# A two-layer transformer trunk: all four column blocks of the down projection by seven products in three blocks of a layer, two blocks' units in one order, one weight sum by adding DMAs

## The chip, the cores and the metric

The kernel runs on one core of one Trainium2 chip. The metric is the device time of one execution in microseconds (us), lower is better. Engines are named as the profile names them: PE (TensorE, matrix products), DVE (VectorE), ACT (ScalarE), POOL (GpSimd) and SP (SyncE, which here only issues DMAs).

## The reference, cut to what matters

256 tokens of width 2048 pass two layers. Each layer is a mixer (attention, not touched here) and an MLP with squared ReLU; the hidden width is 8192, everything is float32.

```python
def sq_relu_mlp(h, w_up, w_down):
    return jnp.square(jax.nn.relu(h @ w_up)) @ w_down

for layer in range(2):
    hn = rms_norm(h, ln_mix_g[layer])
    h = h + mixer(hn, ...)                      # even_mixer, then odd_mixer
    hn = rms_norm(h, ln_mlp_g[layer])
    h = h + sq_relu_mlp(hn, w_mlp_up[layer], w_mlp_down[layer])   # (2048, 8192), (8192, 2048)
```

## The kernel before, in words

**Units and splits.** All weights come as chunks of 1 MB by DMAs that SP issues into three buffers `raw`. A *unit* is 1024 columns of such a buffer, 128 partitions deep. For float32 accuracy each operand is cut into a high and a low part: `split` (L277, L280) lets ACT copy the unit into `wh` and lets DVE subtract, `wl = raw - wh`. PE then forms high·high, high·low and low·high, so that a product takes three matmuls, each 128x128 by 512 columns. There are `NHL` = 4 pairs `wh`, `wl`: unit u+3 is split while PE works on unit u, and ACT can begin that split only when PE has finished unit u-1. An ordinary unit is 12 matmuls.

**The order.** Everything is laid out in a Python list `units`; `run()` emits the units in that order, and between matmuls it lets background tasks (`bg`) emit a piece. Each engine executes its own instructions strictly in the order in which they were emitted, and waits at an instruction whose inputs aren't there. That holds for SP too: a DMA that waits for its buffer holds up every DMA behind it.

**The MLP.** The hidden width goes in eight blocks of 1024. `up_units(b)` makes block b of the hidden layer: 16 ordinary units, two groups g of 512 columns. The result lies token by token in PSUM; `blocks` (L440, DVE) and 16 small DMAs (`across`, L446, 32 KB each, issued by SP, `t<-t`) turn it into the layout that the next product needs; then L892 (DVE) squares the ReLU, and L899 (ACT) and L901 (DVE) cut it into high and low part in `big`.

**The down projection of block b** (0 to 6) is done in two ways. Column blocks 2 and 3 (of four, 512 columns each) by `pair_units(b)`: 8 ordinary units, 96 matmuls. Column blocks 0 and 1 by `seven_units(b)`, a Strassen-Winograd scheme: tokens, hidden rows and columns are halved, and seven products of sums take the place of eight. Each product is two units of 6 matmuls, so 84 matmuls in place of 96. The sums of hidden values are made by `token_sums`. The sums of weights are made in place: four 1 MB buffers (the three `sum` and `sm`) are loaded with the quarters x0, z0, w0, y0 of the weights, and a class `Stage` adds them up as their turn comes: x1 = x0 + w0, x2 = x1 + y0, y1 = y0 + w0, x3 = x2 + z0. Each of these sums is two additions on DVE (L236, 128x1024), one for each unit. A stage keeps the conditions `free` (its buffer may be overwritten), `have` and `used`; `run()` calls `issue` of all stages before each unit. After each of the seven products DVE adds the result to the residual `xs` (L983), of which P and R are PSUM banks 0 and 2 (several products go there one after another), and Q is bank 1.

**The order of a block.** For block b the list takes the 24 ordinary units of `up_units(b)` and `pair_units(b-1)`, and sets the 14 units of `seven_units(b-1)` between them at places `at`: three ordinary units to each product. Block 7 of the down projection is done whole by `down_units`, at the end.

Of the kernel before, what the change touches and what calls it, by code (L numbers as in the profile page):

```python
# [148 lines left out]
def trunk_kernel(ctx: ExitStack, tc: tile.TileContext, x, w_up, w_down, even_w_in, even_w_out,  # L149
# [65 lines left out]
    class Stage:  # L215
# [2 lines left out]

        def __init__(self, buf, free, src=None, add=None, prev=None):
            self.buf, self.free, self.src, self.add, self.prev = buf, free, src, add, prev
# [643 lines left out]
    def mlp(layer, norm, nxt):  # L866
        up, down = w_up[layer], w_down[layer]
        NBLK = DFF // 1024

        def hid(b):  # L870

# [5 lines left out]
        def up_units(b):  # L877
            for g in range(2):
                def evac(hf, ps, g=g):
                    turned_, d = T[g], T[2 + g]  # L880
                    if b:
                        bg.need(heads["hid", b - 1, g])
                    blocks(turned_[:, hf * 512:(hf + 1) * 512], ps)

                    def rest():
                        if b:
                            yield (lambda: heads["sum", layer, b - 1].done)
# [12 lines left out]
                        yield 1  # L900
                        nc.vector.tensor_tensor(lo, q, h, ALU.subtract)  # L901
                        yield 1
                    if hf == 1:
                        heads["hid", b, g] = bg.spawn(rest(), 1)

                a_units(up, [(b * 1024 + g * 512, 512)], xl, list(range(KT)), evac,
                        lambda g=g: (bank[4 + 2 * g], bank[5 + 2 * g]), norm.need)

        def token_sums(b):

            yield (lambda: b == 0 or ("sums", b - 1) in passed)
            x11, x21, x12, x22 = (T[i][:, a:a + 512].rearrange("p (s j t) -> p j s t", s=4, j=4)
                                  for i in (2, 3) for a in (0, 512))
            p, q = SQ
            for i, dst, a, c, op in ((0, p, x21, x22, ALU.subtract), (1, q, p, x11, ALU.subtract),
                                     (3, p, x12, q, ALU.add), (2, q, x11, x21, ALU.subtract)):
                d, a, c = (t.rearrange("p (j s t) -> p j s t", s=4, j=4) if t is p or t is q else t for t in (dst, a, c))
                nc.vector.tensor_tensor(d, a, c, op)  # L920
                yield 2
# [6 lines left out]
        def seven_units(b, first):  # L928

            def w(r, n):
                return down[b * 1024 + r * 512:b * 1024 + r * 512 + 512, n * 512:n * 512 + 512].rearrange("(k p) c -> p k c", p=128)

            bx, by, bz = (summed[(i + 2 * b) % 3] for i in range(3))
            old = kept.get(b - 1)

            def gone(f):

                return f if b else lambda i: current[0] >= start[0] and all(t.done for t in norm.tasks.values())  # L940
# [9 lines left out]
            kept[b] = dict(x1=x1, x3=x3, y1=y1, z0=z0)  # L950
# [10 lines left out]
            P, Q, R = bank[0:3]  # L961
            out_ = []

            for n, (st, lhs, need, o, new, half, col, neg) in enumerate((
                    (x0, hx(0, 0), h0, P, True, 0, 0, 0), (z0, hx(4, 0), hd, Q, True, 0, 0, 0),
                    (x1, sx(0), sm, R, True, 1, 1, 0), (y0, sx(3), sm, R, False, 0, 1, 0),
                    (x2, sx(1), sm, P, False, 0, 1, 1), (y1, sx(2), sm, P, False, 1, 1, 1),
                    (x3, hx(4, 1), hd, P, False, 1, 0, 0))):
                for i in range(2):
                    def gen(u, n=n, i=i, lhs=lhs, need=need, o=o, new=new, half=half, col=col, neg=neg):  # L970
                        bg.need(*need())
                        h, lo = (t[u % NHL].rearrange("p (j c) -> p j c", j=2) for t in (wh, wl))
                        for j in range(2):
                            jj = 2 * i + j
                            nc.tensor.matmul(o, lhs(jj, 0), h[:, j], start=new and jj == 0, stop=False, skip_group_check=True)  # L975
                            nc.tensor.matmul(o, lhs(jj, 0), lo[:, j], start=False, stop=False, skip_group_check=True)  # L976
                            nc.tensor.matmul(o, lhs(jj, 1), h[:, j], start=False, stop=jj == 3, skip_group_check=True)  # L977
                            if jj == 3:
                                xd = xs[:, half, col * 512:col * 512 + 512]
                                f = 2 * neg + half  # L980
                                if b == 0 and n == 0:
                                    bg.need(norm.rtask)
                                nc.vector.scalar_tensor_tensor(xd, o, norm.r2[:, f:f + 1], xd, op0=ALU.mult, op1=ALU.add)  # L983
                                passed.update({("sums", b)} if n == 5 else {("seven", b)} if n == 6 else ())
                            yield

                    out_.append((st, i * 1024, 1024, gen, True))
# [4 lines left out]
        def used(b, g):  # L992

            if b == 0:
                return True
            if b == NBLK - 1:
                return ("sums", b - 1) in passed
            return ("low", b - 1) in passed if g == 0 else {("seven", b - 1), ("eight", b - 1)} <= passed

        start = [None]  # L1000
        kept = {}
# [50 lines left out]

        start[0] = len(units) + 5
        up_units(0)
        for b in range(1, NBLK):
            plain_ = taken(up_units, b) + taken(pair_units, b - 1)
            seven = seven_units(b - 1, b == 1)


            at = (1, 7, 10, 13, 16, 19, 22) if b == 1 else (3, 6, 9, 12, 15, 18, 21)  # L1060
            units.extend(plain_[:at[0]])
            for i, (a, e) in enumerate(zip(at, at[1:] + (len(plain_),))):
# [295 lines left out]
```

## Time and profile before

| | |
|---|---|
| time, median of 3 runs | 2208.41 us (2208.19 to 2209.19) |
| the profiled execution | 2210.6 us, of which the span of its instructions 2208.8 us |
| PE busy | 2201.8 us of the span |
| DVE busy | 1675.4 us |
| ACT busy | 1152.1 us |
| POOL busy | 41.4 us |
| granted TensorE clock | 1.00 |
| the two MLPs in the span | about 455 to 1110 us and 1560 to 2209 us |

The span is the time from the first to the last instruction of the program. A busy PE says only that matmuls follow each other closely; whether one waited is read from the waits and from the chain of work that ended last.

### The profile page before, as it was taken

Reading aid. Unit: us, or ns where it says so; the run is one execution under the profiler, and the core shown is the slowest. Engines: PE = TensorE matmul, PEld = TensorE weight load, DVE = VectorE, ACT = ScalarE, POOL = GpSimd, SP = SyncE. Lnnn points to the kernel's source line nnn. Section 1 sums busy time; section 2 is a strip of 40 time slices with the busy share of each in tenths; the row PEclk is TensorE's granted clock in tenths of the full one; section 3 lists DMA queues with packets and bytes.
Section 4 is the critical chain, followed back from the end, with each engine's and each line's share of the span. In section 5 each row is a group of like instructions: output and inputs, shape, how many; then the busy total and the mean of one; then the engine's idle time right before and its main releaser. Section 6 shows DMA issues by size and latency. Waiting matters only on the chain.

```text
span 2208.8 us, 27276 instructions
## 1 busy us (share of the span) xinstructions
PE 2201.8 (100%) x10037; PEld 1822.5 (83%) x10037; DVE 1675.4 (76%) x2223; ACT 1152.1 (52%) x1471; POOL 41.4 (2%) x28
## 2 busy tenths in 40 slices
PE   9999999999999999999999999999999999999999
PEld 7788888888888888888888888888888888888887
DVE  5676766669888888888764676766788888888885
ACT  5555555545555554555543556555455555545553
POOL 0000000000000000000000000000000000000000
PEclk9999999999999999999999999999999999999999
DMA  8655655686675675675566664535765665765754
GB/s 269 192 190 177 188 182 197 186 274 206 225 243 179 217 247 163 224 238 171 172 194 198 222 201 133 165 110 177 240 232 174 231 227 168 241 227 176 238 171 153
DMA packets 281989, 442.74 MB, mean 200 GB/s; under 512 B 24704, under 2 KB 81280, under 8 KB 281856
## 3 DMA queue, kind: packets, MB, share of 16 engines
q1 hardware_dynamic: 280848, 439.89, 61.1%
q8 instruction: 78, 1.28, 0.2%
q10 hardware_dynamic: 1008, 1.12, 0.1%
q14 instruction: 55, 0.45, 0.1%
HBM read 410.52 MB, written 2.10 MB: 187 GB/s over the span
## 4 chain that ended last, share of the span: by engine, by line
PE 92%; DMA 3%; DVE 2%; SPq 1%; ACT 1%; issue 1%; POOL 0%; DVEq 0%; ACTq 0%
PE bank L376 47%; PE bank L363 8%; PE bank L364 8%; PE bank L365 8%; PE bank L977 4%; PE bank L975 4%; PE bank L976 4%; DMA raw<-in_odd_w_in 2%; PE bank L688 1%; PE bank L720 1%; DVE wl L280 1%; SPq L446 1%; DMA raw<-in_w_up 1%; PE bank L715 1%; PE bank L396 1%; PE bank L397 1%
## 5 line engine op out<-in xcount | busy, mean ns | idle before, releaser
L280 DVE TENSOR_TENSOR wl<-raw,wh 128x1024 fp32r<-128x1024 f32 (+1 forms) x659 | 797.9, 1217 | 313.6 <-ACT wh L277 303.1
L277 ACT ACTIVATE wh<-raw 128x1024 fp32r<-128x1024 f32 (+1 forms) x659 | 691.8, 1055 | 515.8 <-PE bank L376 268.7
L376 PE MATMUL bank<-wh,xT 128*128 128x512 f32 x2592 | 725.6, 391 | 0.0
L376 PEld LDWEIGHTS bank<-wh,xT 128*128 128x128 f32 x2592 | 485.1, 188 | 99.1
L376 PE MATMUL bank<-wl,xT 128*128 128x512 f32 x1296 | 406.3, 391 | 0.6 <-DVE wl L280 0.6
L277 ACT ACTIVATE wh<-sum 128x1024 fp32r<-128x1024 f32 x196 | 207.7, 1060 | 247.6 <-PE bank L376 159.1
L376 PEld LDWEIGHTS bank<-wl,xT 128*128 128x128 f32 x1296 | 243.2, 188 | 51.3 <-DVE wl L280 1.0
L280 DVE TENSOR_TENSOR wl<-sum,wh 128x1024 fp32r<-128x1024 f32 x196 | 238.9, 1219 | 57.3 <-ACT wh L277 57.3
L376 PE MATMUL bank<-wh,big 128*128 128x512 f32 x784 | 222.8, 391 | 0.0
L363 PE MATMUL bank<-wh,big 128*128 128x512 f32 x440 | 175.4, 399 | 0.0
L376 PEld LDWEIGHTS bank<-wh,big 128*128 128x128 f32 x784 | 146.9, 188 | 30.0
L365 PE MATMUL bank<-wh,big 128*128 128x512 f32 x440 | 171.6, 390 | 0.0
L364 PE MATMUL bank<-wl,big 128*128 128x512 f32 x440 | 171.4, 389 | 0.0
L363 PE MATMUL bank<-wh,xT 128*128 128x512 f32 x432 | 170.8, 395 | 0.1
L364 PE MATMUL bank<-wl,xT 128*128 128x512 f32 x432 | 168.4, 390 | 0.3 <-DVE wl L280 0.3
L365 PE MATMUL bank<-wh,xT 128*128 128x512 f32 x432 | 168.3, 390 | 0.0
L977 PE MATMUL bank<-wh,big 128*128 128x512 f32 x392 | 152.6, 389 | 0.0
L975 PE MATMUL bank<-wh,big 128*128 128x512 f32 x392 | 152.5, 389 | 0.0
L976 PE MATMUL bank<-wl,big 128*128 128x512 f32 x392 | 152.5, 389 | 0.0
L376 PE MATMUL bank<-wl,big 128*128 128x512 f32 x392 | 123.2, 392 | 0.0
L365 PEld LDWEIGHTS bank<-wh,big 128*128 128x128 f32 x440 | 82.6, 188 | 17.6 <-DVE big L729 0.2
L363 PEld LDWEIGHTS bank<-wh,big 128*128 128x128 f32 x440 | 82.7, 188 | 16.3 <-ACT big L727 0.2
(218 smaller groups left out, 2165.3 us busy)
## 6 DMA issues: line engine op xcount, KB each, us to landing
raw<-in_w_up SPq DMA_DIRECT2D x128, 1024.0 KB, 6.0
raw<-in_w_down SPq DMA_DIRECT2D x72, 1024.0 KB, 5.3
raw<-in_even_w_in SPq DMA_DIRECT2D x48, 1024.0 KB, 5.2
sum<-in_w_down SPq DMA_DIRECT2D x42, 1024.0 KB, 8.5
raw<-in_odd_w_in SPq DMA_DIRECT2D x40, 1024.0 KB, 5.3
t<-t SPq DMA_DIRECT2D x608, 32.0 KB, 2.9
raw<-in_even_w_out SPq DMA_DIRECT2D x16, 1024.0 KB, 5.2
raw<-in_odd_w_out SPq DMA_DIRECT2D x16, 1024.0 KB, 5.0
```

Source lines behind the costliest of these rows:

```text
L277: nc.scalar.activation(h[:, at], r[:, at], AF.Copy)
L280: nc.vector.tensor_tensor(lo[:, at], r[:, at], h[:, at], ALU.subtract)
L363: nc.tensor.matmul(o, lhs(k, 0, hf), h[:, n], start=st, stop=False)
L364: nc.tensor.matmul(o, lhs(k, 0, hf), lo[:, n], start=False, stop=False)
L365: nc.tensor.matmul(o, lhs(k, 1, hf), h[:, n], start=False, stop=last and n == len(ks) - 1)
L376: nc.tensor.matmul(bks[hf], lhs(k, part, hf), w_[:, n], start=False, stop=False)
L396: nc.tensor.matmul(o, lhs(k, 0, hf), lo[:, at], start=False, stop=False)
L397: nc.tensor.matmul(o, lhs(k, 1, hf), h[:, at], start=False, stop=k == KT - 1)
L446: nc.sync.dma_start(dst[32 * q:32 * q + 32].rearrange("i (s a c) -> i s a c", a=4, c=128)[:, :, a], src[32 * a:32 * a + 32].rearrange("i ( ...
L975: nc.tensor.matmul(o, lhs(jj, 0), h[:, j], start=new and jj == 0, stop=False, skip_group_check=True)
L976: nc.tensor.matmul(o, lhs(jj, 0), lo[:, j], start=False, stop=False, skip_group_check=True)
L977: nc.tensor.matmul(o, lhs(jj, 1), h[:, j], start=False, stop=jj == 3, skip_group_check=True)
```

## The change

- **Seven products for all columns.** In blocks 1, 3 and 5 of a layer (`WIDE`) `seven_units` is called a second time (c = 1) for column blocks 2 and 3, and `pair_units` is left out there. `pair_units` stays for blocks 0, 2, 4 and 6.
- **Turns.** The four buffers are now passed round among all four roles; each call of `seven_units` is a *turn* (10 in a layer, before 7). In turn n+1 x0 is loaded into the buffer that was w0's in turn n.
- **Q stays in PSUM.** The product of z0 is summed up in its bank (1, or 3 for c = 1) over all blocks and added to `xs` once, at the end (`ends`).
- **Two blocks in one order.** For b = 2, 4, 6 the list takes `up_units(b)`, `up_units(b+1)` and `pair_units(b)`, 40 ordinary units, and sets three turns, 42 units, between them: two ordinary units to a product, at four places one.
- **One weight sum by adding DMAs.** y1 = y0 + w0 (`far=True`) is no longer made on DVE: POOL issues a DMA from w0's buffer to y0's with `accum_op=ALU.add`, one for each half (512 KB).
- **The squared ReLU** of blocks 1 to 7 is two ACT instructions (Relu, Square) in place of one on DVE (L892); it is emitted six steps later. `LATER` goes from 5 to 4, and `token_sums` pauses 3 in place of 2 between its steps.

```diff
-    NRAW, NHL, SPACED, LATER = 3, 4, 3, 5
+    NRAW, NHL, SPACED, LATER = 3, 4, 3, 4
...
-                if not self.have[i] and self.free(i) and (must or u >= self.prev.at[i] + LATER):
+                if not self.have[i] and self.free(i) and (must or u >= self.prev.at[i] + (1 if self.far else LATER)):
                     at = slice(i * 1024, i * 1024 + 1024)
-                    nc.vector.tensor_tensor(self.buf[:, at], self.buf[:, at], self.add[:, at], ALU.add)
+                    if self.far:
+                        nc.gpsimd.dma_start(self.buf[:, at], self.add[:, at], accum_op=ALU.add)
+                    else:
+                        nc.vector.tensor_tensor(self.buf[:, at], self.buf[:, at], self.add[:, at], ALU.add)
...
+        WIDE = (1, 3, 5)
...
-                        yield 18 if b else 12
-                        nc.vector.scalar_tensor_tensor(d, d, 0.0, d, op0=ALU.max, op1=ALU.mult)
+                        yield 24 if b else 12
+                        if b == 0:
+                            nc.vector.scalar_tensor_tensor(d, d, 0.0, d, op0=ALU.max, op1=ALU.mult)
+                        else:
+                            nc.scalar.activation(d, d, AF.Relu)
+                            yield 3
+                            nc.scalar.activation(d, d, AF.Square)
...
-            x0 = Stage(bx, gone(lambda i: old["z0"].used[i] and old["x3"].have[i]), src=w(0, 0))
+            x0 = Stage(bx, gone(lambda i: old["x1"].have[i] and old["y1"].have[i]), src=w(0, 0))
             z0 = Stage(bz, gone(lambda i: old["y1"].used[i]), src=w(1, 0))
-            w0 = Stage(smw[:, 0:2048], gone(lambda i: old["x1"].have[i] and old["y1"].have[i]), src=w(0, 1))
+            w0 = Stage(bw, gone(lambda i: old["z0"].used[i] and old["x3"].have[i]), src=w(0, 1))
...
-            y1 = Stage(by, lambda i: y0.used[i] and x2.have[i] and w0.have[i], add=w0.buf, prev=y0)
+            y1 = Stage(by, lambda i: y0.used[i] and x2.have[i] and w0.have[i], add=w0.buf, prev=y0, far=True)
...
-                            if jj == 3:
-                                xd = xs[:, half, col * 512:col * 512 + 512]
+                            if jj == 3 and (n != 1 or ends):
+                                at = (2 * c + col) * 512
+                                xd = xs[:, half, at:at + 512]
...
-        for b in range(1, NBLK):
-            plain_ = taken(up_units, b) + taken(pair_units, b - 1)
-            seven = seven_units(b - 1, b == 1)
+        for b in (1, *range(2, NBLK, 2)):
+            if b > 1:
+                plain_ = taken(up_units, b) + taken(up_units, b + 1) + taken(pair_units, b)
+                seven = seven_units(b - 1, 0) + seven_units(b - 1, 1) + seven_units(b, 0)
+            else:
+                plain_ = taken(up_units, b) + taken(pair_units, b - 1)
+                seven = seven_units(b - 1, 0)
```

How the change moves instructions is seen at three places. First DVE, in the middle of a turn of an inner block of layer 0 (`wl` is a unit's low part, `L236` adds weights, `L983` adds a product to `xs`); before:

```order
L236 TENSOR_TENSOR sum_89<-sum_89,sum_90 128x1024
L280 TENSOR_TENSOR wl_87<-sum_90,wh_83 128x1024
L983 SCALAR_TENSOR_TENSOR xs<-bank_65,r_m_122,xs 128x512
L280 TENSOR_TENSOR wl_84<-raw_77,wh_80 128x1024
L236 TENSOR_TENSOR sum_89<-sum_89,sum_90 128x1024
L280 TENSOR_TENSOR wl_85<-sum_90,wh_81 128x1024
L280 TENSOR_TENSOR wl_86<-raw_77,wh_82 128x1024
L280 TENSOR_TENSOR wl_87<-raw_78,wh_83 128x1024
L236 TENSOR_TENSOR sum_90<-sum_90,sm 128x1024
L892 SCALAR_TENSOR_TENSOR t_93<-t_93 128x1024
L280 TENSOR_TENSOR wl_84<-sum_89,wh_80 128x1024
L983 SCALAR_TENSOR_TENSOR xs<-bank_65,r_m_122,xs 128x512
```

The same part of a turn in the changed kernel (its lines stand a few further down: L239 adds weights, L283 makes `wl`, L1000 adds a product):

```order
L239 TENSOR_TENSOR sum_88<-sum_88,sum_89 128x1024
L283 TENSOR_TENSOR wl_86<-sum_89,wh_82 128x1024
L283 TENSOR_TENSOR wl_87<-raw_79,wh_83 128x1024
L1000 SCALAR_TENSOR_TENSOR xs<-bank_65,r_m_122,xs 128x512
L239 TENSOR_TENSOR sum_88<-sum_88,sum_89 128x1024
L283 TENSOR_TENSOR wl_84<-sum_89,wh_80 128x1024
L283 TENSOR_TENSOR wl_85<-raw_77,wh_81 128x1024
L283 TENSOR_TENSOR wl_86<-sum_88,wh_82 128x1024
L443 STREAM_TRANSPOSE t_91<-bank_67 128x512
L443 STREAM_TRANSPOSE t_91<-bank_68 128x512
L283 TENSOR_TENSOR wl_87<-raw_77,wh_83 128x1024
L1000 SCALAR_TENSOR_TENSOR xs<-bank_65,r_m_122,xs 128x512
```

The additions of y1 (`sum_90<-sum_90,sm`) and the squared ReLU (L892) are gone from DVE, and the units of the turn stand closer together. Second POOL, which had nothing to do between the two norms of layer 0 (`r_m` and `r_a`); in the changed kernel the first adding DMAs stand there, twenty in a layer:

```order
L470 TENSOR_TENSOR r_m_121<-r_m_121,nhalf 128x2
L237 DMA sum_89<-sm 128x1024 x2
L237 DMA sum_88<-sum_90 128x1024 x2
L237 DMA sm<-sum_89 128x1024 x2
L237 DMA sum_90<-sum_88 128x1024 x2
L237 DMA sum_89<-sm 128x1024 x2
```

Each pair is one y1, and each turn has another pair of buffers. Third SP, where x0 of a turn is loaded (`sum2_90`), with the semaphores waited for (DMAHW are landings of SP's own DMAs, DMASW landings of POOL's); before, in block 1 of layer 0:

```order
L229 DMA sum2_90<-in_w_down 128x4x512 [waits DMAHW4_49,DVE_49]
L264 DMA raw0_77<-in_w_up 128x4x512 [waits DMAHW5_49,Activation_49]
L229 DMA sum1_89<-in_w_down 128x4x512 [waits DMAHW6_49,DVE_49]
L264 DMA raw1_78<-in_w_up 128x4x512 [waits DMAHW7_49,DVE_49]
L229 DMA sum0_88<-in_w_down 128x4x512 [waits DMAHW0_49,DVE_49]
```

In the changed kernel x0 of the next turn (the second row) and what stands behind it:

```order
L267 DMA raw0_77<-in_w_up 128x4x512 [waits DMAHW2_49,DVE_49]
L229 DMA sum2_90<-in_w_down 128x4x512 [waits DMAHW6_49,DMASW3_49,DMASW2_49]
L449 DMA t2_93<-t0_91 32x2x128 [waits DVE_49]
L449 DMA t2_93<-t0_91 32x2x128 [waits DMAHW0_49]
L449 DMA t2_93<-t0_91 32x2x128 x2
L267 DMA raw1_78<-in_w_up 128x4x512 [waits DMAHW3_49,DVE_49]
```

SP now waits at x0 for both adding DMAs of the turn before, and the 16 small DMAs of a hidden group and the next chunk of weights stand behind that wait.

## Rows read from the trace of the kernel before

**Rows 1.** The page: span, and busy time of PE.

```profile
span 2208.8 us, 27276 instructions
PE 2201.8 (100%) x10037; PEld 1822.5 (83%) x10037; DVE 1675.4 (76%) x2223; ACT 1152.1 (52%) x1471; POOL 41.4 (2%) x28
```

**Rows 2.** Busy time by stretch: the engines in turn, granted clock, DMA share, GB/s.

```profile
500.00:585.00 85.00, 84.71 (x373) 69.53 (x372) 74.95 (x80) 45.74 (x49) 0.00 (x0) 1.00 0.68 228
755.00:840.00 85.00, 85.00 (x377) 70.41 (x376) 73.27 (x75) 44.55 (x46) 0.00 (x0) 1.00 0.64 210
...
1880.00:1965.00 85.00, 85.00 (x376) 70.38 (x375) 73.27 (x75) 44.80 (x45) 0.00 (x0) 1.00 0.64 214
```

**Rows 3.** All that PE waited for from 500 to 1095 us.

```profile
PE bank L364 <- DVE wl L280: 0.3, 1, 0.3
```

**Rows 4.** The chain that ended last: start, us, what.

```profile
725.66 5.44 PE bank L376 x24
...
1552.20 16.32 PE bank L376 x72
```

**Rows 5.** DVE's groups, 500 to 1095 us: xcount, busy us, mean ns, idle before.

```profile
L280 DVE TENSOR_TENSOR wl<-raw,wh 128x1024 fp32r<-128x1024 f32 x172 | 208.9, 1221 | 51.9 <-ACT wh L277 47.4
L983 DVE SCALAR_TENSOR_TENSOR xs<-bank,r_m,xs 128x512 f32<-128x512 f32 x48 | 35.8, 745 | 0.0
L236 DVE TENSOR_TENSOR sum<-sum,sum 128x1024 f32<-128x1024 f32 x28 | 33.9, 1212 | 0.0
L236 DVE TENSOR_TENSOR sum<-sum,sm 128x1024 f32<-128x1024 f32 x27 | 32.9, 1219 | 0.0
...
L440 DVE STREAM_TRANSPOSE t<-bank 128x512 f32<-128x512 f32 x28 | 18.4, 693 | 0.0
...
L892 DVE SCALAR_TENSOR_TENSOR t<-t 128x1024 f32<-128x1024 f32 x15 | 18.3, 1219 | 2.2 <-DMA t<-t 2.2
```

**Rows 6.** ACT's groups in the same stretch.

```profile
L277 ACT ACTIVATE wh<-raw 128x1024 fp32r<-128x1024 f32 x171 | 180.3, 1059 | 109.3 <-PE bank L376 52.5 <-PE bank L365 24.9 <-PE bank L977 22.6
...
L899 ACT ACTIVATE big<-t 128x1024 fp32r<-128x1024 f32 x15 | 15.7, 1046 | 3.7 <-DVE t L892 3.7
```

**Rows 7.** The timeline around the last matmul of two products.

```profile
640.96 0.39 PE L977 MATMUL bank<-wh,big 128*128 128x512 f32 x1
...
641.11 1.23 DVE L280 TENSOR_TENSOR wl<-sum,wh 128x1024 fp32r<-128x1024 f32 x1 [1.49 <-ACT wh L277]
...
642.26 0.74 DVE L983 SCALAR_TENSOR_TENSOR xs<-bank,r_m,xs 128x512 f32<-128x512 f32 x1
...
651.84 0.39 PE L977 MATMUL bank<-wh,big 128*128 128x512 f32 x1
...
653.93 0.75 DVE L983 SCALAR_TENSOR_TENSOR xs<-bank,r_m,xs 128x512 f32<-128x512 f32 x1
```

**Rows 8.** DMA issues over the whole span: xcount, KB each, median us to landing.

```profile
raw<-in_w_up SPq DMA_DIRECT2D x128, 1024.0 KB, 6.0
...
sum<-in_w_down SPq DMA_DIRECT2D x42, 1024.0 KB, 8.5
...
t<-t SPq DMA_DIRECT2D x608, 32.0 KB, 2.9
...
raw<-in_even_w_in SPq DMA_DIRECT2D x10, 512.0 KB, 5.3
```

**Rows 9.** SP's timeline: start, us that the issues took, what.

```profile
770.50 10.29 SPq L446 DMA_DIRECT2D t<-t  x16
...
810.32 0.53 SPq L264 DMA_DIRECT2D raw<-in_w_up  x1
```

**Rows 10.** What the DMAs moved, 585 to 1095 us in 40 slices.

```profile
GB/s 134 172 176 265 223 375 127 138 118 229 222 376 196 166 183 170 236 206 384 140 166 122 169 270 299 295 166 151 137 215 206 375 180 155 175 181 181 133 223 172
```

More of the change, by code (lines that the diff above doesn't have):

```diff
@@ L215, in trunk_kernel, with __init__ @@
     class Stage:
-        def __init__(self, buf, free, src=None, add=None, prev=None):
-            self.buf, self.free, self.src, self.add, self.prev = buf, free, src, add, prev
+        def __init__(self, buf, free, src=None, add=None, prev=None, far=False):
+            self.buf, self.free, self.src, self.add, self.prev, self.far = buf, free, src, add, prev, far
             self.have, self.used, self.at = [False] * 2, [False] * 2, [0] * 2
@@ L886, in rest @@
                         if b:
-                            yield (lambda: heads["sum", layer, b - 1].done)
+                            yield (lambda: ("sum", layer, b - 1) in heads and heads["sum", layer, b - 1].done)
                         for a in range(4):
@@ L926, in token_sums, with seven_units @@
                 yield 2
-        def seven_units(b, first):
+        def seven_units(b, c):
             def w(r, n):
-                return down[b * 1024 + r * 512:b * 1024 + r * 512 + 512, n * 512:n * 512 + 512].rearrange("(k p) c -> p k c", p=128)
-            bx, by, bz = (summed[(i + 2 * b) % 3] for i in range(3))
-            old = kept.get(b - 1)
+                at = c * 1024 + n * 512
+                return down[b * 1024 + r * 512:b * 1024 + r * 512 + 512, at:at + 512].rearrange("(k p) c -> p k c", p=128)
+            turn = len(kept)
+            places = summed + [smw[:, 0:2048]]
+            bx, by, bz, bw = (places[(i - turn) % 4] for i in range(4))
+            old = kept.get(turn - 1)
+            final = c == 1 or b not in WIDE
             def gone(f):
-                return f if b else lambda i: current[0] >= start[0] and all(t.done for t in norm.tasks.values())
-            x0 = Stage(bx, gone(lambda i: old["z0"].used[i] and old["x3"].have[i]), src=w(0, 0))
+                return f if turn else lambda i: current[0] >= start[0] and all(t.done for t in norm.tasks.values())
+            x0 = Stage(bx, gone(lambda i: old["x1"].have[i] and old["y1"].have[i]), src=w(0, 0))
             z0 = Stage(bz, gone(lambda i: old["y1"].used[i]), src=w(1, 0))
-            w0 = Stage(smw[:, 0:2048], gone(lambda i: old["x1"].have[i] and old["y1"].have[i]), src=w(0, 1))
+            w0 = Stage(bw, gone(lambda i: old["z0"].used[i] and old["x3"].have[i]), src=w(0, 1))
             y0 = Stage(by, gone(lambda i: old["x3"].used[i]), src=w(1, 1))
@@ L947, in seven_units @@
             x2 = Stage(bx, lambda i: x1.used[i] and y0.have[i], add=by, prev=x1)
-            y1 = Stage(by, lambda i: y0.used[i] and x2.have[i] and w0.have[i], add=w0.buf, prev=y0)
+            y1 = Stage(by, lambda i: y0.used[i] and x2.have[i] and w0.have[i], add=w0.buf, prev=y0, far=True)
             x3 = Stage(bx, lambda i: x2.used[i] and z0.have[i], add=bz, prev=x2)
-            kept[b] = dict(x1=x1, x3=x3, y1=y1, z0=z0)
+            kept[turn] = dict(x1=x1, x3=x3, y1=y1, z0=z0)
             def hx(j0, half):
@@ L960, in seven_units @@
             sm = lambda: [heads["sum", layer, b]]
-            P, Q, R = bank[0:3]
+            P, Q, R = bank[0], bank[1 + 2 * c], bank[2]
+            ends = b == (NBLK - 2, WIDE[-1])[c]
             out_ = []
             for n, (st, lhs, need, o, new, half, col, neg) in enumerate((
-                    (x0, hx(0, 0), h0, P, True, 0, 0, 0), (z0, hx(4, 0), hd, Q, True, 0, 0, 0),
+                    (x0, hx(0, 0), h0, P, True, 0, 0, 0), (z0, hx(4, 0), hd, Q, b == c, 0, 0, 0),
                     (x1, sx(0), sm, R, True, 1, 1, 0), (y0, sx(3), sm, R, False, 0, 1, 0),
@@ L976, in gen @@
                             nc.tensor.matmul(o, lhs(jj, 0), lo[:, j], start=False, stop=False, skip_group_check=True)
-                            nc.tensor.matmul(o, lhs(jj, 1), h[:, j], start=False, stop=jj == 3, skip_group_check=True)
-                            if jj == 3:
-                                xd = xs[:, half, col * 512:col * 512 + 512]
+                            nc.tensor.matmul(o, lhs(jj, 1), h[:, j], start=False, stop=jj == 3 and (n != 1 or ends), skip_group_check=True)
+                            if jj == 3 and n == 0 and c == 1:
+                                passed.add(("low", b))
+                            if jj == 3 and (n != 1 or ends):
+                                at = (2 * c + col) * 512
+                                xd = xs[:, half, at:at + 512]
                                 f = 2 * neg + half
@@ L983, in gen @@
                                 nc.vector.scalar_tensor_tensor(xd, o, norm.r2[:, f:f + 1], xd, op0=ALU.mult, op1=ALU.add)
-                                passed.update({("sums", b)} if n == 5 else {("seven", b)} if n == 6 else ())
+                                if final:
+                                    passed.update({("sums", b)} if n == 5 else {("seven", b)} if n == 6 else ())
                             yield
@@ L997, in used @@
                 return ("sums", b - 1) in passed
-            return ("low", b - 1) in passed if g == 0 else {("seven", b - 1), ("eight", b - 1)} <= passed
+            need_ = {("low", b - 1)} if g == 0 else {("seven", b - 1)} if b - 1 in WIDE else {("seven", b - 1), ("eight", b - 1)}
+            return need_ <= passed
         start = [None]
@@ L1054, in mlp @@
         up_units(0)
-        for b in range(1, NBLK):
-            plain_ = taken(up_units, b) + taken(pair_units, b - 1)
-            seven = seven_units(b - 1, b == 1)
-            at = (1, 7, 10, 13, 16, 19, 22) if b == 1 else (3, 6, 9, 12, 15, 18, 21)
+        for b in (1, *range(2, NBLK, 2)):
[5 more added lines that the diff above has]
+                seven = seven_units(b - 1, 0)
+            m = len(seven) // 2
+            if b == 1:
+                at = [1, 7, 10, 13, 16, 19, 22]
+            else:
+                at = [2]
+                for i in range(m - 1):
+                    at.append(at[-1] + (1 if i in (1, 8, 10, 15) else 2))
             units.extend(plain_[:at[0]])
-            for i, (a, e) in enumerate(zip(at, at[1:] + (len(plain_),))):
+            for i, (a, e) in enumerate(zip(at, at[1:] + [len(plain_)])):
                 mine, others = seven[2 * i:2 * i + 2], plain_[a:e]
```

2 lines of the change are left out of this document (1 added, 1 removed).

## The prediction

> **What bounds the kernel now.** I read the busy times first. PE is busy for practically the whole span of 2208.8 us [rows 1]; that alone proves little, so the stretches come next. In the MLP PE is busy 85.00 of 85 us, at granted clock 1.00, while DVE is busy 73.27 us (86%) and ACT about 45 us (53%) [rows 2]. Then the waits: from 500 to 1095 us PE waited once, for 0.3 us [rows 3]. Last the chain of work that ended last: it runs through PE, 24 matmuls in 5.44 us and 72 in 16.32 us [rows 4], so one matmul costs 0.2267 us and nothing stands between them. In the MLP the time is the number of matmuls times 0.2267 us, and a matmul that disappears is worth that, as long as DVE, ACT and the DMAs still keep three units ahead.
>
> **What is removed.** For 512 rows and two column blocks, eight products become seven: 96 matmuls become 84. This is done for one more pair of column blocks in three blocks of two layers: 6 x 12 = 72 matmuls, 72 x 0.2267 = 16.3 us. Two blocks together need 732 matmuls in place of 744: 165.9 us in place of 168.6 us. The weights loaded are the same (four chunks of 1 MB stand for four of `pair_units`).
>
> **What DVE pays.** In two blocks eight units of 12 matmuls become fourteen of 6: six more splits, 6 x 1.22 us; additions of weights go from 16 to 18 (three turns of six, since y1 left), 2 x 1.22 us; four squared ReLUs leave, -4 x 1.22 us; additions of products to `xs` stay at 22, because that of z0 falls away [rows 5]. Sum +4.9 us. DVE goes from 0.862 x 168.6 = 145.4 us to 150.3 us of 165.9 us, 91%. So on average DVE hides the extra work behind PE. Locally it is tighter. A product with its two ordinary units now takes 36 matmuls, 8.16 us; in it DVE has four splits (4.88 us), one addition to `xs` (0.75 us) and, at three of seven products, two weight additions (2.43 us): 8.06 us. Token sums and transposes (0.69 us each) come on top. Before it was 9.3 of 10.9 us. The lead covers that: a split may end three units (at least 24 matmuls, 5.44 us) after it could begin and needs 1.06 us of ACT [rows 6] and 1.22 us of DVE, which leaves 3.2 us. Three crowded products in a row with two transposes each overdraw 3 x 1.3 = 3.9 us, 0.7 us more than that, at most once in a turn, 14 us in twenty turns; the four uncrowded products of each turn (5.63 of 8.16 us) pay it back. I take 0.
>
> **A bank used again sooner.** Products that share a PSUM bank stood two ordinary units apart and now stand one apart, 12 matmuls. DVE must have read the bank by then. At 640.96 us the last matmul of a product begins and its addition ends at 643.00 us, 2.04 us later, with a split directly ahead of it; the other case is 651.84 to 654.68 us, 2.84 us, with more instructions in between [rows 7]. The next product of the bank now begins 13 x 0.2267 = 2.95 us after that last matmul. Both fit. In the order of the changed kernel 90 of the 124 additions follow directly on two splits in a row; the other 34 have two transposes or token sums ahead of the last split. I take 0; if each of the 34 were late by 0.15 us, 5 us.
>
> **ACT** gets 36 more copies of 1.06 us and 56 instructions of about 1.05 us for the squared ReLU [rows 6], +97 us: 1249 us of some 2192, 57%. Its idle time before the copies is waiting for PE (109.3 us in the stretch), which hides it.
>
> **The adding DMAs** are the step for which the trace has no row: call L the time from the end of what they wait for to landing. Below, L is bounded by the small DMAs between SBUF tiles, 2.9 us for 32 KB; above by loads into the same buffers, 8.5 us for 1 MB, times 1.5 for what 512 KB move (two halves read, one written), 12.8 us, or twice 8.5 us, 17 us, if adding goes at half the rate [rows 8]. I take 6 to 8 us, near the 512 KB load (5.3 us) and the 1 MB load (6.0 us), since the DMA engines are busy 64% of the time [rows 2] and have moved 384 GB/s where the mean of these slices is about 200 [rows 10]: 3 MB more in 166 us find room. By the fit in the Trainium skill (DMA: Bandwidth & Descriptors, "Anatomy of one DMA — SWDGE (gpsimd) path"), 2.0 us plus bytes at 436 GB/s, 512 KB would take an estimated 3.2 us, and the sum would be the same.
>
> Two things wait for L. First the split of y1's half. From the adding DMA of the second half to that split the order has four units of 6 and three of 12, 60 matmuls, 13.6 us; the unit is needed 30 matmuls later (6.8 us), less 2.3 us for ACT and DVE: PE stops only if L exceeds 18.1 us. Second SP. The load of the next x0 waits for both halves, and behind it stand the 16 small DMAs of a hidden group (10.3 us of issuing) and a chunk (0.5 us) [rows 9], the last landing 2.9 us after its issue. As SP has eight landing semaphores in turn, the later ones also wait for x0's own landing; in all the last small DMA lands about L + 16 us. The ReLU on ACT waits for it, and behind that the splits. At the places of the fourth and seventh turn of a layer the ReLU stands 96 matmuls (21.8 us) after the adding DMA, and ACT may stand there for 36 more (8.2 us) less 3.3 us of work: L may be 10.6 us. At the three places of the second, fifth and eighth turn the distance is 18 matmuls greater: 14.6 us. x0 itself is needed 25.8 us after, w0 and z0 about 34 us after, and z0 lands by about L + 23 us. With L of 6 to 8 us all of that is hidden.
>
> One rule speaks against putting a DMA on POOL here. DVE is busy for 73.27 of 85 us, with tensor-tensor, scalar-tensor-tensor and transpose instructions, no copies [rows 2, 5]. The Trainium skill (SBUF — State Buffer, "Who interferes with whom") says that DVE in its two-port modes shuts GpSimd out of SBUF, that DMAs issued from GpSimd then stall in writing descriptors, but that a tensor-tensor has no such mode. By its first half the time would be that of the third rival below; by its second half nothing is added, and no run here shows which holds.
>
> **The sum.** -16.3 us, all else hidden. The profiled execution took 2210.6 us and would take 2194.3 us; it lies 2.2 us over the median, so I set the sum against the median: 2208.4 - 16.3 = 2192.1 us. I add 1 us for single waits of the kind of rows 3: 2193 us.
>
> **The rivals.**
> 1. *DVE becomes the bound in the crowded products, or banks come free late*: the 14 us and 5 us above in part, some 4 to 11 us given back, 2196 to 2204 us. For it: 8.06 of 8.16 us. Against it: additions end 0.1 to 0.9 us before they are needed, and a whole turn has 9% to spare.
> 2. *Adding DMAs are slow and hold up SP* (slower than before). Price: 4 places x (L - 10.6) + 6 places x (L - 14.6). At L = 12.8 us that is 9 us, 2201 us; it eats the gain at L = 14.6 us, and at L = 17 us it is 40 us, 2232 us. For it: x0's load stands ahead of the small DMAs, and SP can do nothing else. Against it: no row of 1 MB or less has a median over 8.5 us.
> 3. *DVE holds POOL off.* DVE idles in pieces of about 1.5 us [rows 7] and 14% of the time, so a descriptor batch would wait for up to 1.5 x 0.86 / 0.14 = 9 us: L = 7 + 9 = 16 us, a price of 22 + 8 = 30 us, 2222 us. Against it: the kinds of instructions.
> 4. *Nothing is saved, because PE waited anyway*: 2208 us. Rows 3 exclude that for the MLP; what is left is that several small costs add up to the gain.
>
> **How the numbers follow.** My forecast has 0.63 (2191 to 2196 us), the first rival 0.19, the second 0.09 on its slower side, the third 0.04, the fourth 0.05. A measurement of this kernel can tell 0.2%, 4.4 us, from no change: faster means below 2204.0 us. Faster: 0.63 + 0.19 = 0.82; same: 0.05; slower: 0.09 + 0.04 = 0.13. The range runs from 2191 us (72 matmuls less from the fastest run, 2208.2 us) to 2204 us, the end of the first rival; it holds the second at L = 12.8 us, and leaves out 0.18.
>
> **What would show it.** Right: 72 matmuls less; PE still 100% busy in the MLP and waiting under 3 us in all; two blocks in about 166 us; DVE at about 91%; adding DMAs landing in 6 to 8 us; no idle time of ACT before ReLU over 5 us. Wrong: PE waits on `wl` of a `sum` buffer or behind ReLU (then L was too long, and SP's waits name the adding DMA); PE waits for additions to `xs` (then the banks); DVE without idle time before its splits (then DVE is the bound).

## The result, and the profile after

The changed kernel takes 2193.05 us (median of 6 runs, 2191.8 to 2196.18), the kernel before 2208.84 us beside it (6 runs, 2208.19 to 2209.92): a ratio of 0.9931 [0.9918, 0.9944], 15.8 us less. The forecast was 2193 us, from -16.3 us and +1 us.

The page of the changed kernel: span, and busy time of each engine.

```profile
span 2190.0 us, 27524 instructions
...
PE 2183.5 (100%) x9965; PEld 1808.6 (83%) x9965; DVE 1695.2 (77%) x2241; ACT 1243.7 (57%) x1563; POOL 76.4 (3%) x68
```

PE has 9965 matmuls in place of 10037 [rows 1]: 72 less. The spans differ by 18.8 us, more than 16.3, because part of the difference is not the change's: the first transpose of block 0 of layer 0, which stands behind unchanged code, begins at 465.73 us here and at 467.99 us before, and from that transpose to its like in layer 1 the kernel takes 1072.60 us in place of 1081.05 us. That is 8.4 us for one layer's 36 matmuls, and 36 x 0.2267 us are 8.2 us.

Busy time in the four stretches that hold two blocks in one order (columns as in [rows 2]):

```profile
602.40:768.80 166.40, 166.32 (x734) 137.27 (x733) 149.55 (x152) 101.91 (x102) 5.23 (x6) 1.00 0.75 234
768.80:934.70 165.90, 165.90 (x733) 137.37 (x733) 149.69 (x151) 102.55 (x102) 5.23 (x6) 1.00 0.76 236
1675.70:1841.60 165.90, 165.90 (x733) 137.37 (x733) 149.96 (x151) 102.12 (x102) 5.17 (x6) 1.00 0.76 237
1841.60:2007.50 165.90, 165.90 (x734) 137.37 (x733) 149.97 (x151) 102.38 (x102) 5.17 (x6) 1.00 0.75 235
```

Two blocks take 165.9 us, PE is busy throughout, DVE for 149.7 us of it (90%, before 86%), and the DMA engines are busy 75% of the time (before 64 to 68%). All that PE waited for in the whole program (us in total, times, longest):

```profile
PE bank L203 <- DVE sq L199: 1.5, 1, 1.5
PE bank L398 <- ACT wh L280: 0.6, 1, 0.6
PE bank L399 <- DVE wl L283: 0.5, 1, 0.5
```

None of the three lies in an MLP: from 460 to 1100 us, where [rows 3] had one, and from 1540 us on there is none. DVE's groups from 500 to 1085 us (columns as in [rows 5]):

```profile
L283 DVE TENSOR_TENSOR wl<-raw,wh 128x1024 fp32r<-128x1024 f32 x147 | 179.4, 1222 | 50.9 <-ACT wh L280 50.3
L283 DVE TENSOR_TENSOR wl<-sum,wh 128x1024 fp32r<-128x1024 f32 x102 | 124.4, 1221 | 9.4 <-ACT wh L280 8.2
...
L1000 DVE SCALAR_TENSOR_TENSOR xs<-bank,r_m,xs 128x512 f32<-128x512 f32 x61 | 45.5, 745 | 0.0
```

Ahead of the splits DVE still idles for 60 us, nearly all of it waiting for ACT's copy, so it is not the bound. The two new ACT instructions of the squared ReLU, same stretch: ACT idles for 1.5 us ahead of them, 1.3 us of it for late small DMAs.

```profile
L901 ACT ACTIVATE t<-t 128x1024 f32<-128x1024 f32 x14 | 14.7, 1052 | 0.2
L899 ACT ACTIVATE t<-t 128x1024 f32<-128x1024 f32 x14 | 14.7, 1047 | 1.3 <-DMA t<-t 1.3
```

DMA issues of the whole program (columns as in [rows 8]); those on POOLq are the adding DMAs:

```profile
raw<-in_w_up SPq DMA_DIRECT2D x128, 1024.0 KB, 7.4
...
t<-t SPq DMA_DIRECT2D x608, 32.0 KB, 3.3
...
sum<-sum POOLq DMA_DIRECT2D x20, 512.0 KB, 6.6
sum<-sm POOLq DMA_DIRECT2D x12, 512.0 KB, 6.1
...
sm<-sum POOLq DMA_DIRECT2D x8, 512.0 KB, 6.9
```

An adding DMA lands 6.1 to 6.9 us after its issue (medians by buffer), and with the DMA engines busier than before other transfers take longer (`raw<-in_w_up` 7.4 us, before 6.0; `t<-t` 3.3 us, before 2.9). What SP waited for at x0, 585 to 1080 us, eight turns:

```profile
SPq L229 <- DMA sum<-sum: 39.4, 4, 11.1
...
SPq L229 <- DMA sm<-sum: 21.8, 2, 10.9
SPq L229 <- DMA sum<-sm: 20.5, 2, 11.0
```

SP stands for 9 to 11 us in each of these turns, and PE notices nothing. One such place in SP's timeline: the second adding DMA is issued at 706.38 us and lands at 714.23 us, and at once x0 goes out, then four small DMAs, a chunk of weights (717.36 us), twelve more small DMAs.

```profile
703.36 1.09 SPq L267 DMA_DIRECT2D raw<-in_w_down  x1
714.28 0.37 SPq L229 DMA_DIRECT2D sum<-in_w_down  x1
714.75 2.52 SPq L449 DMA_DIRECT2D t<-t  x4
717.36 0.53 SPq L267 DMA_DIRECT2D raw<-in_w_down  x1
717.93 9.19 SPq L449 DMA_DIRECT2D t<-t  x12
```

ACT in the same place: the chunk landed 5.7 us after its issue, at 723.1 us, and is split from 725.31 us on (ACT waited for PE there, not for the chunk); the ReLU of the hidden group (L899) waited 0.9 us for the small DMAs.

```profile
725.31 1.06 ACT L280 ACTIVATE wh<-raw 128x1024 fp32r<-128x1024 f32 x1 [1.12 <-PE bank L379]
...
728.65 1.06 ACT L899 ACTIVATE t<-t 128x1024 f32<-128x1024 f32 x1 [0.91 <-DMA t<-t]
```

So 2.2 us lie between the chunk's landing and its use. How much this margin is worth became the main question of the experiments.

### The profile page after: what moved, and what is told of

Read it like the earlier page. It is cut to its first block, busy times and chain, and to the rows that moved or that the text cites. A ratio compares the mean times of both kernels' runs of the same rounds, so it can differ in the third digit from the quotient of the medians.

```text
span 2190.0 us, 27524 instructions
## 1 busy us (share of the span) xinstructions
PE 2183.5 (100%) x9965; PEld 1808.6 (83%) x9965; DVE 1695.2 (77%) x2241; ACT 1243.7 (57%) x1563; POOL 76.4 (3%) x68
## 4 chain that ended last, share of the span: by engine, by line
PE 97%; DVE 2%; DMA 1%; ACT 0%; issue 0%; SPq 0%; POOL 0%; DVEq 0%; ACTq 0%
PE bank L379 48%; PE bank L366 8%; PE bank L368 8%; PE bank L367 8%; PE bank L990 6%; PE bank L991 6%; PE bank L989 6%; PE bank L691 1%; PE bank L723 1%; PE bank L718 1%; PE bank L399 1%; DVE wl L283 1%; PE bank L400 1%; PE bank L398 1%; PE bank L1161 0%; DMA raw<-in_odd_w_in 0%
## 5 line engine op out<-in xcount | busy, mean ns | idle before, releaser
L283 DVE TENSOR_TENSOR wl<-raw,wh 128x1024 fp32r<-128x1024 f32 (+2 forms) x611 | 741.4, 1217 | 308.4 <-ACT wh L280 304.8
L280 ACT ACTIVATE wh<-raw 128x1024 fp32r<-128x1024 f32 (+2 forms) x611 | 642.8, 1056 | 555.0 <-PE bank L379 316.5
L280 ACT ACTIVATE wh<-sum 128x1024 fp32r<-128x1024 f32 x208 | 219.9, 1058 | 92.7 <-PE bank L379 50.3
L283 DVE TENSOR_TENSOR wl<-sum,wh 128x1024 fp32r<-128x1024 f32 x208 | 253.5, 1220 | 19.2 <-ACT wh L280 16.4
L990 PE MATMUL bank<-wl,big 128*128 128x512 f32 x560 | 218.0, 389 | 0.1
L366 PE MATMUL bank<-wh,xT 128*128 128x512 f32 x432 | 170.6, 395 | 0.0
L366 PE MATMUL bank<-wh,big 128*128 128x512 f32 x344 | 138.1, 401 | 0.0
L367 PE MATMUL bank<-wl,big 128*128 128x512 f32 x344 | 134.0, 390 | 0.0
L379 PEld LDWEIGHTS bank<-wh,big 128*128 128x128 f32 x592 | 110.9, 188 | 22.5
L990 PEld LDWEIGHTS bank<-wl,big 128*128 128x128 f32 x560 | 105.1, 188 | 22.5 <-DVE wl L283 0.7
L989 PEld LDWEIGHTS bank<-wh,big 128*128 128x128 f32 x560 | 105.1, 188 | 21.8
L991 PEld LDWEIGHTS bank<-wh,big 128*128 128x128 f32 x560 | 105.1, 188 | 21.7
```

The source lines that it names most:

```text
L280: nc.scalar.activation(h[:, at], r[:, at], AF.Copy)
L283: nc.vector.tensor_tensor(lo[:, at], r[:, at], h[:, at], ALU.subtract)
L366: nc.tensor.matmul(o, lhs(k, 0, hf), h[:, n], start=st, stop=False)
L367: nc.tensor.matmul(o, lhs(k, 0, hf), lo[:, n], start=False, stop=False)
L379: nc.tensor.matmul(bks[hf], lhs(k, part, hf), w_[:, n], start=False, stop=False)
```

## The experiments

Three things were open. Is the gain the matmul count and nothing else? The rival: the adding DMA or the ReLU on ACT gives some of it by itself. Is what relieves DVE needed at all, when DVE is busy for 90%? The rival: work that fits under 100% is hidden. And how far is the kernel from the point where the adding DMAs cost something, and where does that cost arise?

### The adding DMA alone, in the kernel before (e1)

```diff
-            y1 = Stage(by, lambda i: ..., add=w0.buf, prev=y0)
+            y1 = Stage(by, lambda i: ..., add=w0.buf, prev=y0, far=True)
...
```

`Stage` gets the branch that issues the adding DMA, as in the change.

> The kernel before, with y1 of its 14 turns made by 28 adding DMAs and nothing else changed. Theory (the time is the number of matmuls, everything else is hidden): no matmul less, so 2208.8 us within 1.5 us, although DVE loses 28 x 1.22 = 34 us of work. Rival (part of the gain came from relieving DVE): 2200 to 2206 us. Rival (adding DMAs cost time by themselves, since SP waits for them before the next load): 2212 us or more.

2209.06 us (11 runs, 2208.43 to 2211.7), ratio 1.0004 [0.9995, 1.0013]. Where PE does not wait, taking two additions a turn off DVE and putting adding DMAs in their place changes nothing that can be told (the interval is -1.1 to 2.9 us).

### The reliefs undone, one by one and together (e2, e3, e4)

In e2 y1 is added up on DVE at the same place, in e3 the squared ReLU is one DVE instruction again, e4 has both edits.

```diff
-                        nc.gpsimd.dma_start(self.buf[:, at], self.add[:, at], accum_op=ALU.add)
+                        nc.vector.tensor_tensor(self.buf[:, at], self.buf[:, at], self.add[:, at], ALU.add)
```

```diff
-                            nc.scalar.activation(d, d, AF.Relu)
+                            nc.vector.scalar_tensor_tensor(d, d, 0.0, d, op0=ALU.max, op1=ALU.mult)
                             yield 3
-                            nc.scalar.activation(d, d, AF.Square)
```

> The changed kernel with y1 added on DVE at the same place of the order, no adding DMA. DVE gets 6 x 1.22 = 7.3 us more in two blocks: 149.7 + 7.3 = 157.0 of 165.9 us, 95%. Theory (a split's lead of three units hides what is under 100%): 2193 to 2196 us. Rival (DVE needed the relief, four crowded products of seven in place of three overdraw the lead): 5 to 15 us more, 2198 to 2208 us.

> The changed kernel with the squared ReLU of blocks 1 to 7 back on DVE, one instruction at the place where Relu stood. DVE gets 4 x 1.22 = 4.9 us more in two blocks: 154.6 of 165.9 us, 93%. Theory (hidden): 2193 to 2195 us. Rival (DVE needed the relief): 2196 to 2203 us.

> The changed kernel with y1 and the squared ReLU both back on DVE: 149.7 + 7.3 + 4.9 = 161.9 of 165.9 us, 98%. Theory (the gain is 72 matmuls, the relief of DVE is what keeps it): at 98% the lead no longer covers the crowded products, some 5 to 15 us are given back, 2198 to 2208 us. Rival (only a DVE busy for more than PE's time costs anything): 2193 to 2195 us.

Against the kernel before: e2 2198.93 us, 0.9960 [0.9947, 0.9972]; e3 2195.88 us, 0.9942 [0.9928, 0.9955]; e4 2202.26 us, 0.9971 [0.9959, 0.9982]. Against the changed kernel's 2193.05 us that is 5.9, 2.8 and 9.2 us more; the interval of e3 overlaps with the changed kernel's, those of e2 and e4 do not. The two costs add up (5.9 + 2.8 = 8.7). What PE waited for in e4, whole program:

```profile
PE bank L988 <- DVE xs L999: 2.7, 6, 0.7
PE bank L366 <- DVE xs L999: 1.7, 2, 0.8
```

The busy times of a two-block stretch in e4:

```profile
600.00:766.00 166.00, 165.79 (x729) 136.71 (x730) 159.47 (x161) 94.69 (x94) 0.00 (x0) 1.00 0.65 216
```

PE waits for the first matmul of a product (L988) whose bank DVE has not yet added to `xs` (L999). The waits of L988 stand alike in e2, those of L366, the first unit of block 7, alike in e3. Read start by start (what lies between the starts of two matmuls beyond 0.2267 us), the gaps in the two MLPs come to 5.1 us in e2, 2.2 us in e3 and 8.7 us in e4, close to the three costs; the profile names a releaser for part of them, but every gap over 0.1 us stands ahead of the first matmul of a product or of block 7. DVE is busy for 154.3 us of 166 (93%) in e3, 156.0 us (94%) in e2 and 159.5 us (96%) in e4: the expectation that work under 100% is hidden falls. e3's time lies between its two expected ranges and can't be told from the changed kernel's; its gaps are what speaks for the rival. What fails is the bank used again sooner, because one more DVE instruction stands ahead of an addition.

### The change in one layer (e5, e6)

e5 is the changed kernel once more, beside e6 to e8 on one chip. In e6 layer 1 has the order of one block at a time again, with `pair_units` in all blocks.

```diff
-        WIDE = (1, 3, 5)
+        WIDE = () if layer else (1, 3, 5)
...
-        for b in (1, *range(2, NBLK, 2)):
-            if b > 1:
+        for b in (1, *range(2, NBLK, 2 if WIDE else 1)):
+            if b > 1 and WIDE:
...
+            elif not WIDE:
+                at = [3, 6, 9, 12, 15, 18, 21]
```

> The changed kernel as it is, so that the next runs have it beside them: 2193.0 us within 1.5 us.

> Seven products for all columns and two blocks in one order in layer 0 alone; layer 1 keeps pair_units in all blocks and one block's order, with the adding DMAs, the ReLU on ACT and the four buffers in turn. Theory (the gain is the number of matmuls): 36 matmuls more than the changed kernel, 8.2 us, 2201.2 us within 1.5 us. Rival (part of the gain comes from the denser order or the relief of DVE): 2197 us or less, or 2204 us or more.

e5: 2193.64 us, 0.9932 [0.9920, 0.9944]. e6: 2202.55 us, 0.9971 [0.9960, 0.9981], 8.9 us more than e5; 36 matmuls are 8.2 us. The gain goes with the matmuls: layer 1 here has the adding DMAs and the ReLU on ACT without a matmul less, and they bring it nothing that can be told.

### The adding DMAs later (e7, e8)

POOL does 26 (e7) or 13 (e8) memsets of a tile that only the mixer uses ahead of each adding DMA; the first instruction multiplies one column of the buffer by 1, so that POOL begins them only when the DMA could have begun.

```diff
+                        nc.gpsimd.tensor_tensor(self.buf[:, at][:, 0:1], self.buf[:, at][:, 0:1], one, ALU.mult)
+                        for _ in range(13):
+                            nc.gpsimd.memset(cs, 0.0)
                         nc.gpsimd.dma_start(self.buf[:, at], self.add[:, at], accum_op=ALU.add)
```

> The changed kernel with a small multiplication by 1 (it takes the waits) and 26 memsets of 311 ns on POOL ahead of every adding DMA: the landing comes some 8.7 us later, L of about 7 us becomes about 15.7 us. Theory of the prediction (SP waits at x0, the small DMAs land late, ReLU holds ACT up; 4 places over 10.6 us and 6 over 14.6 us): 4 x 5.1 + 6 x 1.1 = 27 us more, 2220 us. Rival (SP's wait has more room than that, and only the split of y1 counts, which allows 18.1 us): 2193 to 2195 us.

> The same with 13 memsets: the landing comes some 4.6 us later, L of about 11.6 us. Theory of the prediction: 4 x 1.0 = 4 us more, 2197 us. Rival (more room): 2193 to 2194 us.

e7: 2415.98 us, 1.0938 [1.0923, 1.0953], 222 us over e5. e8: 2234.87 us, 1.0123 [1.0108, 1.0139], 41.2 us over e5. Neither expected figure (2220 and 2197 us, or less by the rival) came near. In both the delay is greater than meant, because the second half's memsets queue behind those of the first. POOL's timeline in e8:

```profile
655.73 1.09 POOL L239 TENSOR_TENSOR sm<-sm,one 128x1 f32<-128x1 f32 x1 [43.58 <-DVE wl L288]
656.76 4.74 POOL L241 MEMSET cs<- 128x256 f32 x13
661.68 0.88 POOL L242 DMA_DIRECT2D sm<-sum  x1 [0.18 <-issue]
...
667.43 0.89 POOL L242 DMA_DIRECT2D sm<-sum  x1
```

x0's load followed at 672.00 us, so the second adding DMA landed about 4.6 us after its issue. Relative to what the two halves wait for, 4 to 5 us apart as in the changed kernel, it is issued about 7 us late: L is about 12 us. By the price in the prediction, 4 x (12 - 10.6), that would cost 5.6 us. It cost 41. The place shown above for the changed kernel, in e8, SP:

```profile
709.16 0.53 SPq L272 DMA_DIRECT2D raw<-in_w_down  x1
724.17 0.37 SPq L231 DMA_DIRECT2D sum<-in_w_down  x1
724.63 2.51 SPq L454 DMA_DIRECT2D t<-t  x4
727.24 0.53 SPq L272 DMA_DIRECT2D raw<-in_w_down  x1
727.82 9.67 SPq L454 DMA_DIRECT2D t<-t  x12
```

And ACT there:

```profile
728.42 1.04 ACT L285 ACTIVATE wh<-sum 128x1024 fp32r<-128x1024 f32 x1
734.43 1.06 ACT L285 ACTIVATE wh<-raw 128x1024 fp32r<-128x1024 f32 x1 [4.97 <-DMA raw<-in_w_down]
735.40 1.04 ACT L285 ACTIVATE wh<-sum 128x1024 fp32r<-128x1024 f32 x1
739.00 1.06 ACT L904 ACTIVATE t<-t 128x1024 f32<-128x1024 f32 x1 [2.56 <-DMA t<-t]
```

SP stood for 14.5 us at x0. The chunk behind it went out at 727.24 us and landed 7.1 us later; ACT, and with it DVE, stood 4.97 us for it, and PE stopped for 2.9 us (from 730 to 740 us it is busy for 7.07 us). At this place, in a fourth turn, the ReLU, of which the prediction took the lateness to count, came after that. In the fifth turn the ReLU is first:

```profile
804.02 1.06 ACT L904 ACTIVATE t<-t 128x1024 f32<-128x1024 f32 x1 [2.02 <-DMA t<-t]
...
807.15 1.23 DVE L288 TENSOR_TENSOR wl<-raw,wh 128x1024 fp32r<-128x1024 f32 x1 [3.90 <-ACT wh L285]
808.30 0.75 DVE L1005 SCALAR_TENSOR_TENSOR xs<-bank,r_m,xs 128x512 f32<-128x512 f32 x1
809.19 0.47 PE L994 MATMUL bank<-wh,big 128*128 128x512 f32 x1 [1.49 <-DVE xs L1005]
```

ACT stood 2.02 us for the small DMAs, DVE stood for ACT at a split, the addition to `xs` stood behind that split, and PE stopped for 1.5 us at the bank, 12 matmuls after the product before. The second and the eighth turn of the layer look the same (ACT 1.2 and 1.3 us, PE 0.8 and 1.0 us), and at the place shown first PE's stop also ends with an addition to `xs`. PE's waits in the whole of e8 name what is late behind ACT, not the DMAs themselves:

```profile
PE bank L994 <- DVE xs L1005: 17.7, 13, 3.1
PE bank L995 <- DVE wl L288: 6.6, 8, 1.2
PE bank L384 <- DVE wl L288: 2.9, 5, 0.7
```

Read start by start, PE's gaps in the two MLPs of e8 come to 38.9 us, nearly all of the 41.2. e7 shows the same at a larger scale: while SP stands the DMA engines run dry, and when it goes on everything comes at once. Two stretches that follow each other (the last three columns: granted clock, DMA share, GB/s):

```profile
680.00:700.00 20.00, 16.43 (x65) 13.09 (x64) 10.45 (x10) 6.79 (x7) 15.71 (x46) 0.87 0.25 57
700.00:720.00 20.00, 17.69 (x72) 13.73 (x71) 16.25 (x18) 12.08 (x13) 0.00 (x0) 0.96 0.93 321
```

The granted clock below 1.00 says that PE, having stood for some of this time, also ran for a part of it at 1.2 in place of 2.4 GHz, so that e7's 222 us are not the waits alone.

### Is it y1's lateness or SP's standing? (e9 to e12)

e9 lets SP issue x0 only four units after the second addition of y1 was emitted, so that other DMAs stand ahead of it in the queue. e11 moves x0's load from SP to POOL, which has nothing to issue behind it. e10 and e12 are e9 and e11 with the 13 memsets of e8.

```diff
-            x0 = Stage(bx, gone(lambda i: old["x1"].have[i] and old["y1"].have[i]), src=w(0, 0))
+            x0 = Stage(bx, gone(lambda i: old["x1"].have[i] and all(old["y1"].have) and current[0] >= old["y1"].did + 4), src=w(0, 0))
...
```

```diff
-                    nc.sync.dma_start(self.buf.rearrange("p (k c) -> p k c", k=4), self.src)
+                    (nc.gpsimd if self.far else nc.sync).dma_start(self.buf.rearrange("p (k c) -> p k c", k=4), self.src)
...
-            x0 = Stage(bx, gone(...), src=w(0, 0))
+            x0 = Stage(bx, gone(...), src=w(0, 0), far=turn > 0)
```

> The changed kernel, with the load of x0 issued four units later, so that the small DMAs and a chunk of weights stand ahead of SP's wait for the adding DMAs and not behind it. PE stood still for only 0.4 us in the MLPs of the changed kernel, so no theory leaves room for a gain: 2193.5 us within 1.5 us. More than 2197 us would say that x0 then comes too late.

> The kernel with 13 memsets ahead of each adding DMA (2234.9 us), and x0 issued four units later. Theory (the 41 us come from what is held up on SP behind the wait at x0): at least half of them go, 2195 to 2214 us. Rival (they come from y1 and x0 themselves being late): 2228 us or more.

> The changed kernel, with the loads of x0 from the second turn on issued by POOL, behind its adding DMAs, so that SP never waits for them. No gain to be had: 2193.5 us within 1.5 us. More than 2197 us would say that a 1 MB load issued by POOL costs more than one by SP.

> The kernel with 13 memsets ahead of each adding DMA (2234.9 us), and x0 issued by POOL: SP isn't held up at all, while y1 and x0 are exactly as late as before. Theory (held up on SP): 2193 to 2205 us. Rival (y1 and x0 themselves late): 2228 us or more.

| | without memsets | with 13 memsets | cost of the lateness |
|---|---|---|---|
| x0 as in the change (e5, e8) | 2193.64, 0.9932 [0.9920, 0.9944] | 2234.87, 1.0123 [1.0108, 1.0139] | 41.2 us |
| x0 issued later (e9, e10) | 2192.56, 0.9936 [0.9921, 0.9951] | 2200.34, 0.9961 [0.9949, 0.9972] | 7.8 us |
| x0 on POOL (e11, e12) | 2194.13, 0.9933 [0.9920, 0.9946] | 2194.40, 0.9934 [0.9922, 0.9946] | 0.3 us |

The three without memsets can't be told apart. With them, e12 has y1 and x0 at least as late as e8 (at the place shown x0 goes out 1.1 us before ACT's split of the chunk before, in e8 2.3 us) and loses nothing; PE's gaps in its two MLPs come to 0.2 us. SP at the same place in e12 has no wait for an adding DMA, and the chunk and the small DMAs go out some 15 us earlier than in e8 (11 us, counted from ACT's split of the chunk before, which begins at 722.27 us here and at 726.50 us there):

```profile
708.38 3.59 SPq L454 DMA_DIRECT2D t<-t  x4
712.06 0.53 SPq L272 DMA_DIRECT2D raw<-in_w_down  x1
712.64 9.06 SPq L454 DMA_DIRECT2D t<-t  x12
```

ACT in e12 does wait for y1 itself, from 600 to 1060 us, but its lead takes that up:

```profile
ACT wh L285 <- DMA sum<-sum: 10.1, 5, 4.3
...
ACT wh L285 <- DMA sum<-sm: 2.9, 2, 2.5
```

So at this lateness the whole cost of a late adding DMA lies in what stands in SP's queue behind the wait, and none that can be told in y1 or x0. No version tried beats the changed kernel by more than the measurement can tell; e11 does the same time and does not depend on L up to 12 us.

## Why the prediction was right, and where its working was not

**The matmuls: right, in mechanism and size.** -16.3 us stood in the sum, 15.8 us were measured (interval of the ratio: 12.4 to 18.1 us), 15.3 us in e5; one layer alone gives its half (e6). Two blocks take 165.9 us, as forecast. The rival that PE waited anyway is out.

**DVE: right in size, by a thinner margin than the text said.** 149.7 of 165.9 us were measured, 150.3 had been worked out, and PE waited for none of it. I had called DVE at 91% hidden "on average" and given the first rival 4 to 11 us. e2 to e4 put that rival on record: it costs 2.8 us (not clear of noise) with DVE at 93%, 5.9 us at 94% and 9.2 us at 96%, not at 100%. The part of it that is real is the banks: PE's waits name additions to `xs`, not splits. In the changed kernel the 53 additions L1000 from 600 to 1060 us end 1.66 us (median) after the end of the product's last matmul; in the same terms the two of [rows 7] are 1.65 and 2.45 us. For 32 of them the bank's next product begins 12 matmuls later, 2.56 us after that end, and the latest of these additions ends after 1.97 us, so 0.6 us are left; the later ones, up to 4.46 us, belong to banks that are used again at least 8 us after that end. So "I take 0" held, and it held because y1 and the ReLU had left DVE; where PE has nothing to wait for (e1, layer 1 of e6) that relief is worth nothing that can be told.

**ACT: right.** 1243.7 us, 57%; worked out were 1249 us.

**L: right in the middle, with a tail.** 6 to 8 us had been taken; the 40 adding DMAs took 4.9 to 10.3 us from issue to landing, and the issue comes about 0.3 us after what it waits for, so L was 5.2 to 10.4 us, 6.8 us in the median. The two longest are in the tenth turn of a layer, behind which no x0 waits. By the fit in the Trainium skill (DMA: Bandwidth & Descriptors, "Anatomy of one DMA — SWDGE (gpsimd) path") they would take an estimated 3.2 us; the medians of 6.1 to 6.9 us, and 4.6 us where SP's queue stood still (e8), are longer, and the measurement decides.

**The price of L: wrong, and it did not show.** This is the step that failed: "behind it stand the 16 small DMAs of a hidden group (10.3 us of issuing) and a chunk (0.5 us)". I counted the chunk for the time of its issue alone and worked out a deadline only for the ReLU behind the small DMAs, which gave L = 10.6 and 14.6 us as the points from which it costs. At the place shown the chunk's own deadline comes first: it has 2.2 us to spare, and the ReLU already waits 0.9 us at L of about 8 us. The ReLU's deadline was set too late as well: "ACT may stand there for 36 more (8.2 us) less 3.3 us of work" counts the lead of the splits, 4.9 us, but an addition to `xs` stands on DVE behind a split that waits for ACT, and PE needs that bank after 12 matmuls. In e8's fifth turn, one of the places put at 14.6 us, ACT stood 2.0 us and PE stopped for 1.5 us at L of about 12 us. At L of about 12 us the kernel loses 41 us and not 5.6; the second rival's break-even, put at 14.6 us, lies below 12 us. Each stand of SP also takes issue time from the chunks and loads that follow (e7's two stretches show it); how e8's 41 us divide between the chunks, the ReLU and this is not shown term by term. The predicted time came out because L was small, and in that respect by luck, not because the margin was as wide as the text had it: the 40 us named for L = 17 us, its own upper bound, are reached at about 12 us.

**DVE holding POOL off: not seen.** POOL spends 0.87 us on an adding DMA (median) and begins it 0.28 us (median; at most 0.53 us) after its release, with DVE busy for 90%. The Trainium skill (SBUF — State Buffer, "Who interferes with whom") says that a tensor-tensor has no two-port mode and, with both inputs in SBUF, contends with GpSimd's reads; the trace agrees in so far as no adding DMA was seen held off beside this mix of instructions. No run has copies on DVE beside these DMAs, so the rule for the two-port modes stays untested.

## What to carry to other kernels

Where PE never waits, a change is worth the matmuls that it takes away, and every relief of another engine is worth only the stall that would otherwise appear. That stall can begin below 100% (here at 93 to 94%): look at the shortest distance between a bank's last matmul and its next use. When a DMA waits for something new, list everything that stands behind it in its issuing engine's queue and work out the deadline of each, down to the place where PE stops: here that was the bank used again soonest, not the lead of the splits. If that list is long, issue the waiting DMA from an engine with an empty queue; it costs nothing here, and the kernel no longer depends on a few microseconds of the awaited transfer.

## What the runs showed of the hardware

An adding DMA of 512 KB between two SBUF buffers takes about as long as a plain load of 512 KB to 1 MB in the same kernel (6.1 to 6.9 us beside 5.5 to 8.8 us), though it reads two operands; these times leave no sign of the factor of 1.5 or 2 for the addition that bounded L from above. With SP's queue standing still it lands in 4.5 to 4.7 us (medians of e7 and e8), which points to the load by other transfers as part of L; no run changes that load alone. Loads of 1 MB that POOL issues into the `sum` and `sm` buffers land after 7.5 and 9.1 us (medians of e11), beside 8.8 and 7.5 us for SP's into the same buffers in the changed kernel: these medians show no disadvantage of either engine.
